# Moving the Newton steps of q's and k's norms to GpSimd and their squares to ScalarE, in a hybrid attention and RG-LRU block

## The chip, the cores and the metric

The kernel runs on one core of a Trainium2 chip. Its engines are TensorE (PE; its weight loads are listed apart as PEld), VectorE (DVE), ScalarE (ACT), GpSimd (POOL) and SyncE (SP), which issues most transfers. The metric is the device time of one execution in microseconds (us), the median over several runs. A profile is one execution recorded instruction by instruction; L92 means line 92 of the kernel.

## The reference

One transformer block over 1024 tokens of width 1024, all in float32. A normed input is projected to q, k, v (8 heads of 64) and to two LRU inputs; q and k are normed head by head; stick-breaking attention and a gated linear recurrence (RG-LRU) run side by side; their results are concatenated, projected and added to x; a squared-ReLU MLP of width 4096 follows.

```python
def rms_norm(x, g):
    xf = x.astype(jnp.float32)
    y = xf * lax.rsqrt(jnp.mean(xf * xf, axis=-1, keepdims=True) + EPS)
    return (y * g.astype(jnp.float32)).astype(x.dtype)

# in hybrid_mixer
    q = rms_norm(q.reshape(B, S, N_ATTN_HEADS, HEAD_DIM), q_norm_g)
    k = rms_norm(k.reshape(B, S, N_ATTN_HEADS, HEAD_DIM), k_norm_g)
    attn = stick_breaking_attention(q, k, v).reshape(B, S, ATTN_WIDTH)
    lru = rg_lru(xl, w_rg, b_rg, w_ig, b_ig, lam) * jax.nn.gelu(gl)
    return jnp.concatenate([attn, lru], axis=-1) @ w_out
# in reference
        x = x + hybrid_mixer(h, ...)
        x = x + sq_relu_mlp(rms_norm(x, norm2_g[l]), w_up[l], w_down[l])
```

## The kernel before

Matrices are split into a high and a low part (`float32r` each), and a product is three matmuls on them (`mm3`, L70 to L73). `lo_part` (L59, L60) makes the low part by a subtraction on VectorE or GpSimd, after a ScalarE cast has made the high part.

The span has these stages. Until about 62 us x is loaded, normed and transposed, and the projections of head pair 0 run. Then come the four column tiles of the LRU branch (`lru_tile`, L364 to L392), with reciprocals (L384) and scans (L391) on VectorE, products (L388, L389) on GpSimd and one Sqrt (L385) a tile on ScalarE, whose table set is loaded and switched back each time. From there to about 460 us a list written out by hand, `ORDER`, interleaves the attention blocks (A and three digits: head pair, head, query chunk of 256), the projections of pairs 1 to 3 (I: pair, token chunk of 256), the gates of the LRU branch (G) and sums of MLP weights by accumulating transfers issued from GpSimd's queue (Y). The output projection and the MLP, behind about 600 us, fill the second half.

The change lies in `in_proj(p, qkv, ws, tp)`, called sixteen times (four pairs, four chunks of 256 tokens). It projects 256 tokens to q, k and v of one head pair (24 matmuls for each 128 tokens). ScalarE evicts q and k to the tile `raw` (L203, two buffers) and v to `vv` (L205); VectorE makes v's low part (L206). Then comes the norm: the squares `sq` (L209) and their sums `ssq` over each head (L211, 8 columns: two token tiles by two heads of q and two of k), `rsqrt_mean` (L88 to L98), the scaling of `raw` (L213), q's gains on GpSimd (L214), and the high and low parts `qs`, `ks`, `kl` (L219 to L223). TensorE transposes these (L228, L233, L237), and ScalarE and VectorE evict them (L229, L234, L238) to `qT`, `kH` and `kL`, which the attention reads.

`rsqrt_mean` computes 1/sqrt(mean + eps) without a table: a first guess from the bits of v (L92, L93) and three Newton steps of three VectorE operations each (L95 to L97), y becoming y(1.5 - 0.5 v y y). Two other places call it, each four times: `norm1_scale` (L250) and the second norm behind the output projection (L602).

In `attention` a block of scores z goes through two sigmoids on ScalarE (L436, L437), a scan on VectorE (L441), a product on GpSimd (L442), transposes on TensorE (L452) and a split (L456, L60), to the matmuls with v (L461).

Within each engine instructions run in the order of its queue. That order is not the order of the text: the kernel is built with `tile.TileContext(nc, schedule_with_timeline_sim=True)`, which plans the queues of all engines from the dependencies and from costs of its own. In the trace, for instance, the Newton steps of one norm lie between steps of another and low parts of x.

Of the kernel before, what the change touches and what calls it, by code (L numbers as in the profile page):

```python
# [13 lines left out]
AF = mybir.ActivationFunctionType  # L14
ALU = mybir.AluOpType
# [9 lines left out]
HD = 64  # L25
# [18 lines left out]
def kernel(ctx, tc, x, norm1_g, w_in, conv_w, conv_b, w_rg, b_rg, w_ig, b_ig,  # L44
                             lam, q_norm_g, k_norm_g, w_out, norm2_g, w_up, w_down, out):
    nc = tc.nc
# [12 lines left out]
    def lo_part(eng, lo, src, hi):  # L59
        ins = eng.tensor_tensor(lo, src, hi.bitcast(F32), op=ALU.subtract)  # L60
        if eng is nc.gpsimd:
            mark(ins)
# [7 lines left out]
    def mm3(ps, ah, al, bh, bl, start, stop):  # L70
        nc.tensor.matmul(ps, al, bh, start=start, stop=False)  # L71
        nc.tensor.matmul(ps, ah, bl, start=False, stop=False)  # L72
        nc.tensor.matmul(ps, ah, bh, start=False, stop=stop)  # L73
# [10 lines left out]
    def bank(pl, shape, name):  # L84
        return pl.tile([P] + shape, F32, tag=pl.name, name=name)


    def rsqrt_mean(ssq, n, cols):  # L88
        v = small.tile([P, 8], F32, tag="rs_v", name="rs_v")[:, :cols]
        y = small.tile([P, 8], F32, tag="rs_y", name="rs_y")[:, :cols]  # L90
        m = small.tile([P, 8], F32, tag="rs_m", name="rs_m")[:, :cols]
        nc.vector.tensor_scalar(v, ssq, 1.0 / n, EPS, op0=ALU.mult, op1=ALU.add)  # L92
        nc.vector.tensor_scalar(y.bitcast(I32), v.bitcast(I32), -0.5, float(0x5F3759DF), op0=ALU.mult, op1=ALU.add)  # L93
        for _ in range(3):
            nc.vector.scalar_tensor_tensor(m, y, -0.5, v, op0=ALU.mult, op1=ALU.mult)  # L95
            nc.vector.tensor_tensor(m, m, y, op=ALU.mult)
            nc.vector.scalar_tensor_tensor(y, m, 1.5, y, op0=ALU.add, op1=ALU.mult)  # L97
        return y  # L98
# [94 lines left out]
    def in_proj(p, qkv, ws, tp):  # L193
        qT, kH, kL, vv = qkv
        raw = mp.tile([P, 2, 4, HD], F32, tag="raw", name=f"raw{p}{tp}", bufs=2)
        for tt in range(2):
            t = 2 * tp + tt
            pd = bank(ps_d, [384], f"pd{p}{t}")
            for kc in range(KC):
                wh, wl = ws[kc]  # L200
                mm3(pd, hTh[:, kc, t * P:(t + 1) * P], hTl[:, kc, t * P:(t + 1) * P], wh, wl, kc == 0, kc == KC - 1)
            rs = rstd1[:, t:t + 1]
            nc.scalar.mul(raw[:, tt].rearrange("p a d -> p (a d)"), pd[:, 0:256], rs)  # L203
            pvv = pd[:, 256:384].rearrange("p (h d) -> p h d", h=2)
            nc.scalar.mul(vv[:, t, :, 0:HD], pvv, rs)  # L205
            nc.vector.scalar_tensor_tensor(vv[:, t, :, HD:P], pvv, rs, vv[:, t, :, 0:HD].bitcast(F32), op0=ALU.mult, op1=ALU.subtract)  # L206
        sq = mp.tile([P, 8, HD], F32, tag="sq", name=f"sq{p}{tp}")
        raw8 = raw.rearrange("p t a d -> p (t a) d")
        nc.vector.tensor_tensor(sq, raw8, raw8, op=ALU.mult)  # L209
        ssq = small.tile([P, 8], F32, tag="ssq8", name=f"ssq{p}{tp}")  # L210
        nc.vector.tensor_reduce(ssq, sq, axis=AX.X, op=ALU.add)  # L211
        rstd = rsqrt_mean(ssq, HD, 8)
        nc.vector.tensor_tensor(raw8, raw8, rstd.unsqueeze(2).broadcast_to([P, 8, HD]), op=ALU.mult)  # L213
        nc.gpsimd.tensor_tensor(raw[:, :, 0:2, :], raw[:, :, 0:2, :], qkg, op=ALU.mult)  # L214
        qs = mp.tile([P, 2, 2, 2, HD], F32R, tag="qs", name=f"qs{p}{tp}")
        ks = mp.tile([P, 4, 2, HD], F32R, tag="ks", name=f"ks{p}{tp}")
        kl = mp.tile([P, 2, 2, HD], F32R, tag="kl", name=f"kl{p}{tp}")
        for h in range(2):
            nc.scalar.copy(qs[:, :, h, h, :], raw[:, :, h, :])  # L219
            lo_part(nc.vector, qs[:, :, h, 1 - h, :], raw[:, :, h, :], qs[:, :, h, h, :])  # L220
        for tt in range(2):
            nc.scalar.copy(ks[:, 2 * tt:2 * tt + 2], raw[:, tt, 2:4, :].unsqueeze(2).broadcast_to([P, 2, 2, HD]))
            lo_part(nc.gpsimd, kl[:, tt], raw[:, tt, 2:4, :], ks[:, 2 * tt:2 * tt + 2, 0, :])  # L223
        cols = slice(256 * tp, 256 * tp + 256)
        pq = bank(ps_t, [2, 256], f"pq{p}{tp}")
        for h in range(2):
            for tt in range(2):
                nc.tensor.matmul(pq[:, h, tt * P:(tt + 1) * P], qs[:, tt, h].rearrange("p a d -> p (a d)"), identr, start=True, stop=True)  # L228
        nc.scalar.copy(qT[:, :, cols], pq)  # L229
        pk = bank(ps_t, [2, 256], f"pk{p}{tp}")  # L230
        for h in range(2):
            for tt in range(2):
                nc.tensor.matmul(pk[:, h, tt * P:(tt + 1) * P], ks[:, 2 * tt + h].rearrange("p a d -> p (a d)"), identr, start=True, stop=True)  # L233
        nc.vector.tensor_copy(kH[:, :, cols], pk)  # L234
        pl = bank(ps_t, [256], f"pl{p}{tp}")
        for tt in range(2):
            nc.tensor.matmul(pl[:, tt * P:(tt + 1) * P], kl[:, tt].rearrange("p a d -> p (a d)"), identr, start=True, stop=True)  # L237
        nc.vector.tensor_copy(kL[:, cols], pl)  # L238
# [11 lines left out]
    def norm1_scale(t0, t1):  # L250
        ssq = small.tile([P, 8], F32, tag="ssq8", name=f"ssq_x{t0}")
        for t in range(t0, t1):
            junk = xp.tile([P, D], F32, tag="junk", name=f"junk{t}", bufs=2)
            nc.scalar.activation(junk, xts[t], AF.Square, accum_out=ssq[:, t - t0:t - t0 + 1])
        nc.vector.tensor_copy(rstd1[:, t0:t1], rsqrt_mean(ssq[:, :t1 - t0], D, t1 - t0))
# [39 lines left out]
    norm1_scale(2, 4)  # L295
    scale_row(0)
    in_proj(0, qkv0, wpair, 0)
    vrow = xp.tile([40, P], F32, name="vrow", bufs=1)
    nc.sync.dma_start(vrow[0:16], conv_w.rearrange("o k (c p) -> (o k c) p", p=P))
# [39 lines left out]
    for tp in range(2, NT // 2):  # L339
        load_x(2 * tp)  # L340
        load_x(2 * tp + 1)
        norm1_pair(2 * tp)
        norm1_scale(2 * tp, 2 * tp + 2)
        if tp == 3:
            scale_row(1)
        in_proj(0, qkv0, wpair, tp - 1)
    in_proj(0, qkv0, wpair, NT // 2 - 1)
    xstack.close()

# [212 lines left out]
    for n in range(2):  # L562
        wo = {}
        for grp in ((0, 1, 2), (3,), (4,), (5,), (6,), (7,)) if n == 0 else tuple((t,) for t in range(NT)):
# [20 lines left out]
            for t in grp:  # L585
                nc.sync.dma_start(x1[:, t, 512 * n:512 * n + 512], x[t * P:(t + 1) * P, 512 * n:512 * n + 512])
                xs = x1[:, t, 512 * n:512 * n + 512]
                nc.vector.tensor_tensor(xs, pos[t], xs, op=ALU.add)
                if n == 1 and t % 2:
                    for b in range(KC // 2):  # L590
                        pt = bank(ps_w, [2, 2, P], f"pth{t}_{b}")
                        for j in range(2):
                            for i in range(2):
                                nc.tensor.transpose(pt[:, j, i, :], x1[:, t - 1 + i, (2 * b + j) * P:(2 * b + j + 1) * P], ident)
                        for j in range(2):
                            kc = 2 * b + j
                            nc.scalar.mul(h2[:, kc, (t - 1) * P:(t + 1) * P], pt[:, j].rearrange("p i t -> p (i t)"), gain2[:, kc:kc + 1])
                    ssq = small.tile([P, 8], F32, tag="ssq8", name=f"ssq_h{t}")
                    for i in range(2):
                        junk = stp.tile([P, 2, 512], F32, tag="sl", name=f"junkh{t}{i}")  # L600
                        nc.scalar.activation(junk.rearrange("p a b -> p (a b)"), x1[:, t - 1 + i, :], AF.Square, accum_out=ssq[:, i:i + 1])
                    rstd = rsqrt_mean(ssq[:, :2], D, 2)  # L602
                    nc.vector.tensor_tensor(rs2[:, t - 1:t + 1], rstd, rstd, op=ALU.mult)
# [271 lines left out]
```

## Time and profile before

| | us |
|---|---|
| median of 3 runs | 1215.21 |
| lowest and highest | 1215.03 and 1216.63 |
| the profiled execution | 1218.14 |
| its span (first to last instruction) | 1216.4 |

The span is what the profile's positions in time are counted from; the time around it is 1.74 us. The mean clock that TensorE was granted is 0.969 of full speed. In a group's row stand the line, the engine, the operation, output and inputs with their shapes, the count; then busy us and mean ns of one; then the idle time of the engine just before these instructions and what ended it. In the row of a source line three durations stand for least, median and most. "Issue" in the chain of waits is time in which an engine waited for nothing that the profile shows. In a row of the timeline or of the chain the first number is the start, the second the duration.

### The profile page before, as it was taken

What the parts mean: (1) busy time and instruction counts of PE and PEld (TensorE: products, weight loads), DVE (VectorE), ACT (ScalarE), POOL (GpSimd) and SP (SyncE); (2) the same over time, 40 slices, a digit from 0 to 9 for tenths busy, and PEclk for the clock granted to TensorE, in tenths of its full rate; (3) what the DMA queues carried; (4) which work ended last, traced back from release to release, by engine and by line L of the source; (5) the groups of instructions that cost most, each with busy time, mean ns of one, the idle gap of its engine ahead of it and who ended that gap; (6) DMA issues with size and microseconds to landing.
All of it is one profiled execution on the core that took longest, in us unless ns stands there. A gap on an engine that the chain in (4) does not pass through costs nothing.

```text
span 1216.4 us, 15273 instructions
## 1 busy us (share of the span) xinstructions
PE 1150.6 (95%) x5410; PEld 948.0 (78%) x5410; DVE 897.3 (74%) x1182; ACT 568.5 (47%) x991; POOL 586.5 (48%) x472
## 2 busy tenths in 40 slices
PE   7998899999999988998999989889999999999998
PEld 7976777789987766886888767678887887878887
DVE  6889997999898788226387769685843876699663
ACT  7554475665665564144433554233334335733331
POOL 1356764574355566102645746533317368483240
PEclk9999999799999978998999989989999999999999
DMA  8110026824505275200453788944412345442531
GB/s 262 48 49 35 18 96 130 227 66 145 122 5 112 89 256 181 101 1 35 141 188 130 201 241 287 224 142 139 141 35 87 122 144 191 158 148 73 193 132 69
DMA packets 91659, 157.05 MB, mean 129 GB/s; under 512 B 8848, under 2 KB 27328, under 8 KB 91584
## 3 DMA queue, kind: packets, MB, share of 16 engines
q1 hardware_dynamic: 79040, 122.54, 30.5%
q0 software_dynamic: 12544, 33.56, 11.8%
q8 instruction: 42, 0.69, 0.2%
q14 instruction: 33, 0.27, 0.1%
HBM read 145.58 MB, written 44.04 MB: 156 GB/s over the span
## 4 chain that ended last, share of the span: by engine, by line
PE 69%; DVE 13%; issue 8%; DMA 3%; POOL 3%; ACT 3%; SPq 0%; DVEq 0%; ACTq 0%; POOLq 0%
PE p L633 22%; PE pa L633 11%; PE pb L633 5%; PE pc L633 4%; PE pd L71 3%; PE pd L72 3%; PE pd L73 3%; PE po L71 3%; PE po L72 2%; PE po L73 2%; PE av L461 2%; PE z L432 2%; PE pw L452 2%; DVE g L441 2%; DVE sl_u L60 2%
## 5 line engine op out<-in xcount | busy, mean ns | idle before, releaser
L442 POOL TENSOR_TENSOR w<-w,g 128x128 f32<-128x128 f32 (+3 forms) x96 | 99.7, 1044 | 107.7 <-DVE g L441 52.7
L60 DVE TENSOR_TENSOR ml_p<-rp,mh_p 128x1024 fp32r<-128x1024 f32 x56 | 110.3, 1971 | 28.1 <-ACT mh_p L544 28.1
L441 DVE TENSOR_TENSOR_SCAN g<-g 128x128 f32<-128x128 f32 (+3 forms) x96 | 112.6, 1185 | 8.0 <-ACT g L436 5.4
L544 ACT CAST sh_p<-U 128x1024 fp32r<-128x1024 f32 x48 | 50.5, 1051 | 131.0 <-PE pa L633 59.2
L633 PE MATMUL pa<-mh_p,sl_p 128*128 128x512 f32 x256 | 100.7, 393 | 7.1 <-DVE sl_p L60 6.8
L767 POOL TENSOR_TENSOR rp<-rp,qp 128x1024 f32<-128x1024 f32 x24 | 69.0, 2876 | 70.3 <-DMA qp<-in_w_down_dram 39.8
L633 PE MATMUL pa<-ml_p,sh_p 128*128 128x512 f32 x256 | 100.3, 392 | 0.0
L633 PE MATMUL pa<-mh_p,sh_p 128*128 128x512 f32 x256 | 100.1, 391 | 0.0
L71 PE MATMUL pd<-wh_p,hTl 128*128 128x384 f32 x256 | 90.9, 356 | 7.3 <-DVE vv L206 5.0
L72 PE MATMUL pd<-wl_p,hTh 128*128 128x384 f32 x256 | 89.8, 351 | 0.1
L73 PE MATMUL pd<-wh_p,hTh 128*128 128x384 f32 x256 | 88.3, 345 | 0.0
L60 DVE TENSOR_TENSOR sl_p<-U,sh_p 128x1024 fp32r<-128x1024 f32 x38 | 63.4, 1668 | 30.7 <-ACT sh_p L544 30.7
L737 POOL TENSOR_TENSOR ru<-ru,rv 128x1024 f32<-128x1024 f32 x16 | 43.8, 2769 | 58.9 <-DMA rv<-sum_u 58.8
L544 ACT CAST mh_p<-rp 128x1024 fp32r<-128x1024 f32 x56 | 58.7, 1048 | 21.3 <-POOL rp L767 14.6
L633 PEld LDWEIGHTS pa<-mh_p,sl_p 128*128 128x128 f32 x256 | 48.5, 189 | 18.2 <-DVE sl_p L60 7.5
L662 POOL TENSOR_TENSOR U<-U 128x512 f32<-128x512 f32 x32 | 47.0, 1501 | 32.0 <-ACT U L660 32.0
L456 ACT CAST wth<-pw 128x512 fp32r<-128x512 f32 (+1 forms) x80 | 42.4, 545 | 38.0 <-PE pw L452 24.8
L436 ACT ACTIVATE g<-z 128x384 f32<-128x384 f32 (+3 forms) x96 | 47.8, 497 | 22.9 <-PE z L434 10.4
L71 PEld LDWEIGHTS pd<-wh_p,hTl 128*128 128x128 f32 x256 | 49.4, 193 | 11.0 <-DVE vv L206 6.7
L660 ACT ACTIVATE U<-U 128x512 f32<-128x512 f32 x48 | 30.0, 628 | 58.6 <-DVE U L721 31.1
L60 DVE TENSOR_TENSOR wtl<-pw,wth 128x512 fp32r<-128x512 f32 (+1 forms) x80 | 49.5, 629 | 9.5 <-ACT wth L456 8.9
L633 PEld LDWEIGHTS pa<-mh_p,sh_p 128*128 128x128 f32 x256 | 48.5, 189 | 10.2
(325 smaller groups left out, 3566.7 us busy)
## 6 DMA issues: line engine op xcount, KB each, us to landing
sum_u<-in_w_up_dram POOLq DMA_DIRECT2D x8, 2048.0 KB, 12.7
sum_d<-in_w_down_dram POOLq DMA_DIRECT2D x8, 2048.0 KB, 13.3
rp<-in_w_down_dram SPq DMA_DIRECT2D x32, 512.0 KB, 4.1
rp<-sum_d SPq DMA_DIRECT2D x24, 512.0 KB, 5.4
ra<-in_w_up_dram SPq DMA_DIRECT2D x16, 512.0 KB, 4.4
qp<-in_w_down_dram SPq DMA_DIRECT2D x16, 512.0 KB, 4.2
wr_p<-in_w_in_dram SPq DMA_DIRECT2D x24, 192.0 KB, 5.8
xt<-in_x_dram SPq DMA_DIRECT2D x8, 512.0 KB, 7.5
```

Source lines behind the costliest of these rows:

```text
L60: ins = eng.tensor_tensor(lo, src, hi.bitcast(F32), op=ALU.subtract)
L71: nc.tensor.matmul(ps, al, bh, start=start, stop=False)
L72: nc.tensor.matmul(ps, ah, bl, start=False, stop=False)
L73: nc.tensor.matmul(ps, ah, bh, start=False, stop=stop)
L436: nc.scalar.activation(g[:, :kn], z, AF.Sigmoid, scale=-1.0)
L441: nc.vector.tensor_tensor_scan(gr, gr, gr, g[:, kn:kn + 1], op0=ALU.mult, op1=ALU.bypass)
L442: mark(nc.gpsimd.tensor_tensor(w[:, :kn], w[:, :kn], g[:, 1:kn + 1], op=ALU.mult))
L544: nc.scalar.copy(hl[0], src)
L633: nc.tensor.matmul(ps, x_, y_, start=start and n == 0, stop=stop and n == 2, skip_group_check=True)
L662: mark(nc.gpsimd.tensor_tensor(c, c, c, op=ALU.mult))
L737: mark(nc.gpsimd.tensor_tensor(r, r, q, **add))
L767: mark(nc.gpsimd.tensor_tensor(r, r, q, **add))
```

## The change

`rsqrt_mean` gets a flag. With it the first guess stays on VectorE, v is scaled by -0.5 in place on GpSimd, and each Newton step is four plain GpSimd operations in place of three VectorE ones, two of which fuse two operations. Only the call in `in_proj` sets the flag. The squares of `raw` in `in_proj` become one ScalarE activation.

```diff
-    def rsqrt_mean(ssq, n, cols):
+    def rsqrt_mean(ssq, n, cols, gp=False):
...
         nc.vector.tensor_scalar(v, ssq, 1.0 / n, EPS, op0=ALU.mult, op1=ALU.add)
         nc.vector.tensor_scalar(y.bitcast(I32), v.bitcast(I32), -0.5, float(0x5F3759DF), op0=ALU.mult, op1=ALU.add)
+        if gp:
+            nc.gpsimd.tensor_scalar(v, v, -0.5, 0.0, op0=ALU.mult, op1=ALU.add)
+            for _ in range(3):
+                nc.gpsimd.tensor_tensor(m, y, y, op=ALU.mult)
+                nc.gpsimd.tensor_tensor(m, m, v, op=ALU.mult)
+                nc.gpsimd.tensor_scalar(m, m, 1.0, 1.5, op0=ALU.mult, op1=ALU.add)
+                nc.gpsimd.tensor_tensor(y, y, m, op=ALU.mult)
+            return y
         for _ in range(3):
             nc.vector.scalar_tensor_tensor(m, y, -0.5, v, op0=ALU.mult, op1=ALU.mult)
...
-        nc.vector.tensor_tensor(sq, raw8, raw8, op=ALU.mult)
+        nc.scalar.activation(sq, raw8, AF.Square)
         ssq = small.tile([P, 8], F32, tag="ssq8", name=f"ssq{p}{tp}")
         nc.vector.tensor_reduce(ssq, sq, axis=AX.X, op=ALU.add)
-        rstd = rsqrt_mean(ssq, HD, 8)
+        rstd = rsqrt_mean(ssq, HD, 8, True)
```

## The prediction

> **What bounds the kernel now.** I read the busy shares of the page first, then the busy time of each engine by stretches, then the chain of work that ended last inside the stretches where TensorE isn't full.
>
> ```profile
> span 1216.4 us, 15273 instructions
> ...
> PE 1150.6 (95%) x5410; PEld 948.0 (78%) x5410; DVE 897.3 (74%) x1182; ACT 568.5 (47%) x991; POOL 586.5 (48%) x472
> ```
> ```profile
> 100.00:150.00 50.00, 41.01 (x189) 32.74 (x188) 49.48 (x51) 24.86 (x38) 32.45 (x26) 0.99 0.08 32
> ...
> 250.00:300.00 50.00, 50.00 (x305) 44.25 (x303) 47.42 (x90) 30.63 (x75) 31.22 (x39) 1.00 0.34 114
> ...
> 350.00:400.00 50.00, 48.28 (x272) 40.10 (x271) 42.90 (x84) 29.37 (x76) 29.12 (x46) 0.97 0.34 70
> ...
> 600.00:1216.00 616.00, 589.98 (x2557) 483.64 (x2556) 429.11 (x322) 244.69 (x286) 300.15 (x131) 0.98 0.49 153
> ```
>
> The columns of a stretch are its ends, its length, then the busy time of PE, PEld, DVE, ACT and POOL, the granted clock, and DMA. Over the whole span TensorE is the bound, but the change touches only the sixteen norms of q and k, which run before 400 us; the 616 us behind 600 hold none of them and I count no change there. What matters is how the norms' stretches differ. From 250 to 300 TensorE is busy for all 50 us: DVE work taken away there buys nothing. From 100 to 150 it is VectorE that is full (49.48 of 50) while TensorE is busy for 41.01; from 350 to 400 TensorE has 1.7 us idle and fewer weight loads (271 against 303). In the first 62 us, where the four norms of pair 0 lie, I also count nothing: what they wait for is work that TensorE's own projections and transposes cover. So a gain has to come from the LRU stretch (to about 155 us) and the attention stretches around 180 and 360 to 390.
>
> **The change part by part: what leaves VectorE.**
>
> ```profile
> L209 DVE TENSOR_TENSOR sq<-raw 128x512 f32<-128x512 f32 x16 | 14.4, 901 | 4.7 <-ACT raw L203 4.7
> ...
> L96 DVE TENSOR_TENSOR rs_m<-rs_m,rs_y 128x8 f32<-128x8 f32 x48 | 12.4, 260 | 0.9
> ...
> L97 DVE SCALAR_TENSOR_TENSOR rs_y<-rs_m,rs_y 128x8 f32<-128x8 f32 x48 | 11.4, 238 | 0.9
> ...
> L95 DVE SCALAR_TENSOR_TENSOR rs_m<-rs_y,rs_v 128x8 f32<-128x8 f32 x48 | 10.1, 212 | 0.9
> ```
>
> Sixteen squares (14.4 us) and 144 Newton operations (12.4 + 11.4 + 10.1 = 33.9 us) leave: 48.3 us of DVE busy time. The two operations that prepare v and y (L92, L93) and the reduction (L211) stay on VectorE. Only what stands on the chain counts:
>
> ```profile
> 130.99 1.43 issue
> ...
> 144.83 0.06 DVE rs_m L96
> 144.89 1.03 issue
> ...
> 147.06 1.16 DVE rs_y L97
> 148.21 0.60 DVE sq L209
> ...
> 151.62 0.20 DVE rs_m L95 x2
> 151.82 0.20 DVE rs_m L96 x2
> 152.02 0.20 DVE rs_y L97 x2
> ```
> ```profile
> 174.62 0.87 DVE sq L209
> ...
> 181.10 0.14 DVE rs_m L95
> ...
> 183.89 0.18 DVE rs_y L97
> ```
> ```profile
> 361.59 0.65 DVE sq L209
> ...
> 365.25 1.91 DVE g L441
> ...
> 367.45 0.97 DVE rs_m L96
> ...
> 369.05 0.18 DVE rs_y L97
> ...
> 380.21 1.08 issue
> ...
> 383.36 0.18 DVE rs_m L95
> ...
> 385.99 1.01 DVE g L441
> 387.00 0.06 DVE rs_y L97
> ```
>
> These are rows of the chain (start, us, what). The "issue" at 130.99 lies inside a square and that at 144.89 inside an L96. (1) LRU stretch: squares 1.43 + 0.60, with small pieces 2.2 us; Newton 0.06 + 1.03 + 1.16, with small pieces 2.5 us. Here the chain follows VectorE's queue: the LRU's reciprocals and scans stand behind these operations, so what leaves is gained. (2) 174 to 184: square 0.87; nine Newton operations from 181.10 to 183.89, 1.5 us, nearly back to back, each waiting for the one before. (3) 361 to 369: square 0.65, Newton 2.05 (the 0.97 in it). (4) 380 to 387: square 1.1, Newton 1.2 in nine pieces from 383.36 to 387.00, with other DVE work (the scan of 1.01 and evictions) between them. With the second Newton chain of the LRU stretch, 0.20 + 0.20 + 0.20 us at 151.62 and small pieces, 0.7 in all, that is 4.8 us of squares and 8.0 us of Newton, 12.8 us at most, in six norms.
>
> **What ScalarE gets.**
>
> ```profile
> L385 ACT ACT_TABLE_LOAD x4 | 5.1, 1283 | 0.1
> ...
> L488 ACT ACTIVATE ge<-gx 128x512 f32<-128x512 f32 x8 | 5.0, 631 | 8.2 <-DVE gx L487 7.7 <-POOL w L442 0.4
> ```
>
> L488 is a Square of just this shape: 0.63 us, sixteen times 10.1 us, on an engine that is busy for 24.86 of 50 us in the LRU stretch and 29.37 around 375. The reduction now waits for ScalarE instead of for DVE's square: where the chain goes through the norm itself, (2), (3) and (4), 0.63 us comes back each time, 1.9 us. Behind a Square on ScalarE stand the sigmoids of the next attention block; 0.63 us is covered by its idle half. In the LRU stretch ScalarE switches table sets (1283 ns a load); no Square of the trace runs under the Sqrt's set, so a reload is possible there, a rival below. The Trainium skill, "ScalarE: Activation LUTs", section "Table sets", says that cheap functions such as copy and identity stand in every set, and doesn't name Square among them; by it the reload is unlikely, and no run so far shows it.
>
> **What GpSimd gets.** Per norm 13 operations of 128x8: one scaling of v, then three steps of three products and one addition; 208 in all. None is in the trace.
>
> ```profile
> L404 POOL COPY ext<-ext x4: 187/187/627, 66.4 to 113.0; 128x3 f32<-128x3 f32 x4
> ```
> ```profile
> L442 POOL TENSOR_TENSOR w<-w,g 128x128 f32<-128x128 f32 x16 | 8.3, 520 | 16.1 <-DVE rs_y L97 7.6 <-DVE g L441 3.8 <-DVE rs_m L95 2.3
> ```
> ```profile
> 127.26 1.28 POOL L388 TENSOR_TENSOR rg<-rg,ext 128x512 f32<-128x512 f32 x1 [1.45 <-DVE ext L384]
> 128.62 1.29 POOL L389 TENSOR_TENSOR ig<-ig,rg 128x512 f32<-128x512 f32 x1
> ```
>
> Lower bound 0.187 us (three columns, one input, the median), upper 0.52 us (128 columns, two inputs, the mean). Eight columns are nearer to three, so I take 0.26 us, between that median and the mean of the four copies, (3 x 187 + 627)/4 = 297 ns. A dependent operation starts 0.08 us after the end of its source (127.26 + 1.28 = 128.54, then 128.62). A chain of 13 is 13 x (0.26 + 0.08) = 4.4 us, with the ends 3.5 and 7.8; busy 54 us in sixteen norms, beside POOL's 32.45 of 50 in the LRU stretch. On DVE the same chain took from 1.7 us (nine at 0.18 and the small gaps, back to back) upward.
>
> The upper end has a mechanism:
>
> ```profile
> 144.56 1.42 POOL L388 TENSOR_TENSOR rg<-rg,ext 128x512 f32<-128x512 f32 x1 [2.25 <-DVE rs_m L95]
> ...
> 144.75 1.25 DVE L96 TENSOR_TENSOR rs_m<-rs_m,rs_y 128x8 f32<-128x8 f32 x1
> ```
>
> An operation on 8 columns takes 1.25 us because it overlaps a GpSimd product; the same line's neighbours cost 0.18 elsewhere. This is why the Newton steps hurt DVE, and it works in the other direction too: a small GpSimd operation that meets a DVE scan can wait for it. The Trainium skill, "SBUF — State Buffer", section "Who interferes with whom", says that a DVE instruction with two SBUF inputs and a GpSimd one that reads SBUF exclude each other for the whole instruction, whoever is first. By it each of thirteen operations may wait for one scan, which speaks against this change; the trace agrees from DVE's side.
>
> New waits: GpSimd's first Newton operation waits for DVE's L93, and behind it in GpSimd's queue stand the attention's products (L442), the LRU's L388 and L389 and the issues of the weight sums. DVE's scaling L213 now waits for GpSimd; behind it in DVE's queue stand scans, lo parts and evictions, for which TensorE waits. The order within each queue comes from a planner, so where L213 ends up is not readable here.
>
> **The sum.** (1) 2.2 + 2.5 less what GpSimd's own LRU products are pushed back: its idle gap of 2.25 us (row at 144.56) takes half of a 4.4 us chain, the rest may delay L388; I take 1.0. Gain 3.7. (2) and (3): the chain is the norm's own dependency; DVE gives 1.5 and 2.05 away and is free for its next work, GpSimd answers later; I take nothing. (4) DVE has other work between its pieces: 1.2 + 1.1 - 0.63 = 1.7. Together 5.4 us. The profiled execution took 1218.14 us (span 1216.4 and 1.74 around it), so 1212.7 like it; the median of the three runs is 2.93 lower, so **1209.8, say 1210 us**.
>
> **The rivals.**
> - *The relief comes in full*: DVE always has other work while GpSimd iterates: 12.8 - 1.9 = 10.9 us, 1204. For it: DVE is full in the LRU stretch and a scan of 1.91 us stands between Newton pieces at 365.25. Against: the back-to-back run to 183.89, where it had nothing else.
> - *Given back*: at (2) and (3) the norm's own latency decides and GpSimd's chain is 4.4 - 1.7 = 2.7 us longer each: 5.4 - 5.4 = 0, 1215.
> - *Slower: DVE's queue stands at L213.* Where L213 is put right behind L93, DVE idles for GpSimd's whole chain, 4.4 us, with scans and evictions behind it. In all six norms that is 26.4 - 10.9 = 15.5 us lost, in four 17.6 - 10.9 = 6.7, 1222. It decides from 10.9/4.4 = 2.5 norms on; a chain of 7.8 us needs only 1.4 norms. For it: an in-order queue and a chain over twice as long. Against: in the order before, at (4), other DVE work lies between dependent operations (the scan of 1.01 at 385.99), so the planner fills such waits.
> - *A table reload*: two Squares in the Sqrt's set, two loads each: 4 x 1.28 = 5.1 us, the gain is gone, 1215.
>
> **How the numbers follow.** Forecast (1206 to 1212) 0.40, full relief 0.13, given back 0.20, standing queue 0.22, reload 0.05. A measurement of this kernel tells 0.2% (2.4 us) from no change, so faster is 0.40 + 0.13 = 0.53, same 0.20 + 0.05 = 0.25, slower 0.22. The range reaches below the full relief and just past the standing queue in four norms: 1201 to 1223. The far end, 1231, is left out.
>
> **What would show it.** Right: DVE busy near 850 us, POOL near 640, ACT near 579; the stretch 100 to 150 with TensorE over 43; L213 seldom idle for GpSimd; small GpSimd operations at 0.2 to 0.3 us; the time from L92 to L213 not longer than before. Wrong: DVE idle ahead of L213 released by GpSimd, several us in sum; means near 0.5 us; L442 or TensorE's weight loads waiting for Newton lines; more table loads; or a reordering by the planner that moves the idle time of TensorE in stretches that the change doesn't touch.

## The result and the profile after

The changed kernel takes **1226.81 us** in the median of four runs (1224.53 to 1231.76), the kernel before 1215.12 us on the same chip: a ratio of 1.0100, with a 95% interval of 1.0066 to 1.0134. It is slower by 11.7 us, where 1210 us was forecast. The profiled execution took 1228.02 us (span 1226.2).

The page of the changed kernel, span and busy times:

```profile
span 1226.2 us, 15289 instructions
...
PE 1151.0 (94%) x5410; PEld 948.0 (77%) x5410; DVE 867.1 (71%) x1022; ACT 576.2 (47%) x1007; POOL 641.6 (52%) x680
```

VectorE has 160 instructions less, but only 30.2 us less busy time (897.3 before), not 48.3: some of what is left on it became longer, the scaling of `raw` for one (865 ns in the mean, 691 before). POOL and ACT are where the prediction put them. The same four stretches as in the prediction (ends, length, then busy PE, PEld, DVE, ACT, POOL, clock, DMA):

```profile
100.00:150.00 50.00, 41.73 (x174) 33.19 (x173) 49.03 (x46) 26.93 (x41) 35.96 (x40) 0.88 0.08 32
250.00:300.00 50.00, 48.04 (x282) 40.91 (x281) 39.50 (x63) 30.16 (x71) 40.49 (x66) 1.00 0.21 70
350.00:400.00 50.00, 50.00 (x282) 40.91 (x281) 39.55 (x60) 31.86 (x81) 38.15 (x76) 1.00 0.33 63
600.00:1216.00 616.00, 590.33 (x2559) 484.38 (x2558) 428.09 (x319) 246.49 (x289) 299.61 (x134) 0.98 0.50 154
```

From 100 to 150 VectorE is as full as before, though squares and Newton steps have left it; TensorE's granted clock is 0.88 there instead of 0.99, and its busy time holds fewer matmuls (174, before 189). And from 250 to 300, where TensorE had no idle time at all, it now has 2 us. New groups of the changed kernel between 20 and 470 us (the lines of `in_proj` stand 8 higher than before: L217 is the Square, L221 the scaling of `raw`; L95 scales v on GpSimd, L97 to L100 are the steps), and behind them the scaling in the kernel before:

```profile
L99 POOL TENSOR_SCALAR rs_m<-rs_m 128x8 f32<-128x8 f32 x48 | 13.9, 290 | 3.2
L221 DVE TENSOR_TENSOR raw<-raw,rs_y 128x512 f32<-128x512 f32 x16 | 13.8, 865 | 13.2 <-POOL rs_y L100 12.8 <-POOL g L443 0.3
...
L217 ACT ACTIVATE sq<-raw 128x512 f32<-128x512 f32 x16 | 10.3, 647 | 0.0
L95 POOL TENSOR_SCALAR rs_v<-rs_v 128x8 f32<-128x8 f32 x16 | 7.3, 459 | 25.2 <-DVE rs_y L93 23.5 <-DVE sp L341 1.4
```
```profile
L213 DVE TENSOR_TENSOR raw<-raw,rs_y 128x512 f32<-128x512 f32 x16 | 11.1, 691 | 0.3
```

Two waits are new: VectorE stands 13.2 us at the scaling (0.3 before), GpSimd 25.2 us at the first step. GpSimd's is in part idle time that stood elsewhere, since ahead of the attention's product w it fell from 107.7 to 61.6 us. And the chain of waits, which in the kernel before ran through VectorE's Newton steps, now runs through GpSimd's:

```profile
162.28 0.14 DVE rs_v L92
...
163.51 0.08 DVE rs_y L93
...
164.82 0.11 POOL rs_m L97
164.93 1.07 POOL w L450
166.00 0.29 POOL rs_m L98
...
167.75 1.21 POOL rs_m L99
...
170.16 0.20 POOL rs_y L100
```

This norm, the seventh of sixteen, takes 8.1 us from L92 to its scaling at 170.40; in the kernel before it took 5.6 (161.62 to 167.23). The attention's product (w) stands between the steps in the planner's order, and one step of 0.20 us takes 1.21. In the last twelve norms the steps take 4.2 to 13.1 us from first to last, 7.0 in the mean; the prediction had 4.4, at most 7.8. A good place to measure the stretch as a whole is its last eviction of the attention's output (kernel before, then changed kernel; durations least, median, most, then first and last start):

```profile
L467 DVE TENSOR_TENSOR ob<-av,ot x32: 386/422/428, 169.7 to 461.5; 64x256 f32<-64x256 f32 x32
```
```profile
L475 DVE TENSOR_TENSOR ob<-av,ot x32: 387/422/429, 172.8 to 467.2; 64x256 f32<-64x256 f32 x32
```

So 5.7 of the 9.8 us between the two spans are lost before 468 us. The rest comes after it, where the change has no instruction and all queues have the same order in both kernels: 754.9 us from that eviction to the end before, 759.0 after. Over all 17 profiled executions of this study, whatever the kernel, this remainder lies between 754.6 and 759.7 us. I read the 4 us as that spread; what makes it was not tried. The granted clock doesn't explain the first part: from 0 to 450 us it is 0.96 in both kernels, and in the runs below it doesn't go with the time (e5: 0.94, attention over at 460.3; e6: 0.96, at 486.6).

### The profile page after: what moved, and what is told of

It is laid out like the page before. It is cut to its first block, busy times and chain, and to the rows that moved or that the text cites. A ratio compares the mean times of both kernels' runs of the same rounds, so it can differ in the third digit from the quotient of the medians.

```text
span 1226.2 us, 15289 instructions
## 1 busy us (share of the span) xinstructions
PE 1151.0 (94%) x5410; PEld 948.0 (77%) x5410; DVE 867.1 (71%) x1022; ACT 576.2 (47%) x1007; POOL 641.6 (52%) x680
## 3 DMA queue, kind: packets, MB, share of 16 engines
q0 software_dynamic: 12544, 33.56, 11.7%
## 4 chain that ended last, share of the span: by engine, by line
PE 67%; DVE 12%; issue 8%; POOL 5%; ACT 4%; DMA 4%; SPq 0%; DVEq 0%; POOLq 0%; ACTq 0%
PE p L641 21%; PE pa L641 11%; PE pb L641 5%; PE pc L641 4%; PE po L71 2%; PE av L469 2%; PE po L72 2%; PE po L73 2%; PE pw L460 2%; PE pd L71 2%; PE pd L73 2%; PE pd L72 2%; PE z L440 2%; DVE g L449 1%; DVE sl_p L60 1%
## 5 line engine op out<-in xcount | busy, mean ns | idle before, releaser
L450 POOL TENSOR_TENSOR w<-w,g 128x128 f32<-128x128 f32 (+3 forms) x96 | 100.6, 1059 | 61.6 <-DVE g L449 27.8
L60 DVE TENSOR_TENSOR ml_p<-rp,mh_p 128x1024 fp32r<-128x1024 f32 x56 | 112.8, 2015 | 27.5 <-ACT mh_p L552 27.5
L552 ACT CAST mh_p<-rp 128x1024 fp32r<-128x1024 f32 x56 | 58.6, 1047 | 24.9 <-POOL rp L775 17.3
L670 POOL TENSOR_TENSOR U<-U 128x512 f32<-128x512 f32 x32 | 46.6, 1491 | 31.1 <-ACT U L668 31.1
L60 DVE TENSOR_TENSOR wtl<-pw,wth 128x512 fp32r<-128x512 f32 (+1 forms) x80 | 49.2, 626 | 14.3 <-ACT wth L464 13.6
L460 PE MATMUL pw<-ident,w 128*128 128x128 f32 x288 | 49.7, 293 | 7.4 <-DVE wtl L60 6.2
## 6 DMA issues: line engine op xcount, KB each, us to landing
sum_d<-in_w_down_dram POOLq DMA_DIRECT2D x8, 2048.0 KB, 12.7
```

The lines of the kernel that those rows point to most:

```text
L450: mark(nc.gpsimd.tensor_tensor(w[:, :kn], w[:, :kn], g[:, 1:kn + 1], op=ALU.mult))
L460: nc.tensor.transpose(pw[:, i * P:(i + 1) * P], wrow[rr][j // 4][:, j % 4 * P:(j % 4 + 1) * P], ident)
L552: nc.scalar.copy(hl[0], src)
L670: mark(nc.gpsimd.tensor_tensor(c, c, c, op=ALU.mult))
```

## The experiments

Since the planner places every instruction anew when a kernel changes, a difference of times mixes two things: the operations and the order. To part them, most of the kernels here were given a fixed order: an edge "issue after" (no wait, no semaphore) from each instruction to its neighbour in its engine's queue, for all five engines, with the order of the kernel before, or of the changed one, taken from its built program. In their traces the instructions of VectorE, ScalarE, GpSimd and SyncE that both kernels share do stand in that order.

```diff
+def _pin(tc, nc, mybir, orders):
...
+            if prev is not None:
+                tc.add_manual_dep(seq[at], prev.name, mybir.DependencyInfo(mybir.DependencyClass.NoSync, mybir.DependencyReason.DATA), reason="order")
+            prev = seq[at]
...
         tile_hybrid_block_kernel(tc, *args)
+        _pin(tc, nc, _mybir, _ORDERS)
```

All results in one table. "Old" is the queue order of the kernel before, "new" that of the changed kernel, "free" the planner's own for that kernel. A GpSimd chain in the old order stands together where the norm's first VectorE step stood ("early") or its last ("late"). The kernel before, timed beside each group, had medians of 1214.34 to 1216.9 us; so kernels of different groups are compared by their ratios, and the last but one column is the ratio less 1, times 1216 us. The last eviction is that of the one profiled execution.

| run | square; Newton operations a norm | order | median us | ratio to before (95%) | us against before | last eviction, us |
|---|---|---|---|---|---|---|
| before | VectorE; 9 VectorE | old | 1215.12 | | 0 | 461.5 |
| after | ScalarE; 13 GpSimd | free = new | 1226.81 | 1.0100 (1.0066 to 1.0134) | +12.2 | 467.2 |
| e1 | ScalarE; 13 GpSimd, early | old | 1228.45 | 1.0100 (1.0074 to 1.0127) | +12.2 | 471.2 |
| e2 | VectorE; 9 VectorE | new | 1242.91 | 1.0235 (1.0208 to 1.0261) | +28.6 | 488.6 |
| e3 | ScalarE; 9 VectorE | free | 1242.56 | 1.0235 (1.0209 to 1.0261) | +28.6 | 486.1 |
| e4 | VectorE; 13 GpSimd | free | 1246.69 | 1.0256 (1.0226 to 1.0286) | +31.1 | 488.1 |
| e5 | ScalarE; 9 VectorE | old | 1216.25 | 0.9989 (0.9966 to 1.0011) | -1.3 | 460.3 |
| e6 | VectorE; 13 GpSimd, late | old | 1248.66 | 1.0259 (1.0231 to 1.0288) | +31.5 | 486.6 |
| e7 | ScalarE; 13 GpSimd, late | old | 1241.16 | 1.0205 (1.0178 to 1.0233) | +24.9 | 482.7 |
| e8 | as before, two copies swapped | free | 1229.30 | 1.0112 (1.0081 to 1.0144) | +13.6 | 473.3 |
| e9 | ScalarE; none | old | 1208.45 | 0.9959 (0.9941 to 0.9978) | -5.0 | 453.2 |
| e10 | ScalarE; 5 GpSimd, late | old | 1212.96 | 0.9976 (0.9957 to 0.9994) | -2.9 | 457.0 |
| e11 | ScalarE; 6 VectorE | old | 1214.45 | 0.9971 (0.9950 to 0.9992) | -3.5 | 455.3 |
| e12 | as e7, scaling on GpSimd too | old | 1244.41 | 1.0238 (1.0221 to 1.0256) | +28.9 | 486.8 |
| e13 | ScalarE; 9 GpSimd, late | old | 1225.01 | 1.0071 (1.0045 to 1.0098) | +8.6 | 466.2 |
| e14 | ScalarE; 5 GpSimd | free | 1221.27 | 1.0036 (1.0016 to 1.0056) | +4.4 | 461.2 |
| e15 | ScalarE; none | free | 1222.66 | 1.0048 (1.0029 to 1.0068) | +5.8 | 465.3 |

### Operations against order: e1 and e2

Edit: the fixed order alone, added to the changed kernel (e1) and to the kernel before (e2).

> All of the changed kernel's operations, held on every engine in the queue order that the kernel before had: each Square stands where VectorE's square stood, the 13 GpSimd steps of a norm stand together where its nine VectorE steps began; every other instruction keeps its place (the kernel before's 5394 TensorE, 967 ScalarE, 470 GpSimd, 397 SyncE and 1022 remaining VectorE entries, none moved). Theory A (the operations cost: VectorE stands at the scaling of raw for 13 blocked GpSimd steps, 12.8 us of such waits in the trace of after): this kernel is as slow as the changed one or slower, 1222 to 1232 us, and VectorE shows 10 us or more of waits for GpSimd ahead of that line. Theory B (the planner's new order costs, not the operations): 1206 to 1214 us, what the prediction summed for an order that stays. Half of each: about 1217 to 1221 us.

> All of the kernel before's operations (squares and Newton steps on VectorE), held on every engine in the queue order that the changed kernel had: each norm's nine VectorE steps stand together at the place of its first GpSimd step, the square at that of the Square. Theory A (the operations cost): the time of the kernel before, 1212 to 1218 us. Theory B (the order costs): the time of the changed kernel, 1222 to 1232 us, or more, since VectorE has 30 us more to do in an order that was made for less.

Both theories hold, and they don't add up. With the order kept, the operations cost 12.2 us (and VectorE stands 18.0 us at the scaling). With the operations kept, the new order, made for other operations, costs 28.6 us. Both together cost 12.2: the new order is bad for the old operations, and for the new ones as good as the old. In e1 one sees what a chain on another queue does. Timeline of e1, VectorE, GpSimd and ScalarE:

```profile
153.19 0.69 DVE L221 TENSOR_TENSOR raw<-raw,rs_y 128x512 f32<-128x512 f32 x1
153.38 0.56 POOL L95 TENSOR_SCALAR rs_v<-rs_v 128x8 f32<-128x8 f32 x1 [2.43 <-DVE rs_y L93]
...
157.00 0.20 POOL L100 TENSOR_TENSOR rs_y<-rs_y,rs_m 128x8 f32<-128x8 f32 x1
157.16 0.72 POOL L222 TENSOR_TENSOR raw<-raw,qkg 128x256 f32<-128x256 f32 x1
157.84 0.87 POOL L60 TENSOR_TENSOR kl<-raw,ks 128x128 fp32r<-128x128 f32 x2
157.91 0.50 ACT L227 CAST qs<-raw 128x128 fp32r<-128x128 f32 x2 [3.29 <-POOL raw L222]
```

The scaling at 153.19 belongs to one norm, the thirteen steps behind it to the next. The first norm's gains (L222) stand in GpSimd's queue behind the second norm's chain and come at 157.16; its cast `qs` has waited 3.29 us for them.

### The halves, with a free order and with the old one: e3 to e6

> The squares on ScalarE alone, the Newton steps back on VectorE, the planner free. 16 squares of 900 ns leave VectorE, 16 of 647 ns come to ScalarE; no wait for GpSimd is added. Theory A: 1211 to 1215 us, and the loss of the change is all in its other half. Theory B (order): the planner moves the order again, and the time may land anywhere between 1208 and 1230 us, with no relation to what was moved.

> The Newton steps on GpSimd alone, the squares back on VectorE, the planner free. Theory A: the whole loss is here, 1222 to 1230 us, with VectorE waiting for GpSimd ahead of the scaling of raw for about 12 us in all. Theory B: the planner moves the order in another way, and the time may land anywhere between 1208 and 1230 us; with an order as good as before's it is 1212 to 1216 us.

Edits: in the changed kernel the flag taken away (e3) or the square put back on VectorE (e4).

```diff
-        rstd = rsqrt_mean(ssq, HD, 8, True)
+        rstd = rsqrt_mean(ssq, HD, 8)
```
```diff
-        nc.scalar.activation(sq, raw8, AF.Square)
+        nc.vector.tensor_tensor(sq, raw8, raw8, op=ALU.mult)
```

Each half costs more than the whole, and more than either theory gave it: 28.6 and 31.1 us. Taken alone, e3 would say that the Square is ruinous. Held in the old order the two halves say something else.

> The squares on ScalarE alone, and every queue held in the order of the kernel before; each Square stands at the place of the square that it replaces. Theory B' (a new order alone made the square-only kernel of the first four runs 28 us slower; the Square itself costs nothing): 1209 to 1216 us. Theory A' (the Square on ScalarE is itself what costs): 1225 us or more.

> The Newton steps on GpSimd alone, every queue held in the order of the kernel before; a norm's 13 GpSimd steps stand where its last VectorE step stood, so behind all that GpSimd did before then, and VectorE's scaling of raw keeps its place. Theory A' (each norm comes later by the GpSimd chain of about 3.6 us, against some 1.5 to 2 us for nine VectorE steps, and what waits for it waits too): 1222 to 1230 us. Theory B' (only orders cost): 1208 to 1216 us.

The Square costs nothing that can be measured: a ratio of 0.9989 (0.9966 to 1.0011). All of e3's 28.6 us are its order. The Newton steps are not free: 31.5 us with the order kept, more than Theory A' said; and in e4, the same operations in the planner's own order, they cost as much (31.1).

### Where the chain stands in GpSimd's queue, and how long it is: e7, e10, e13, e9

> All of the changed kernel's operations in the order of the kernel before, as in the first run, but each norm's 13 GpSimd steps stand at the place of its last VectorE step rather than of its first. In the first run's trace one norm's chain stood in GpSimd's queue ahead of the previous norm's multiplication by the gains, which came 4.2 us later for it at 158 us. If the first run's 14 us came from such places in the queue: 1208 to 1218 us. If they come from the chain's length itself (theory A'): 1222 to 1230 us.

> The three Newton steps of q's and k's norms are left out (so their scale is only the first guess); Squares on ScalarE, every queue in the order of the kernel before. Beside the run with the Squares alone (1216.25 us) it takes 9 VectorE steps out of each of 16 norms and puts nothing in their place: what relieving VectorE of them is worth at most. By the prediction's terms, 8.0 us of Newton work on the path: about 1208 us. If that work lies beside other work: 1213 to 1217 us.

> As the seventh run (13 GpSimd steps a norm, at the place of the last VectorE step, 1241.16 us), but with one Newton step in place of three, so 5 GpSimd operations a norm; two steps are left out of the computation. Theory C (the length of the chain on each norm's path costs): between the run without steps (Z) and the seventh in proportion to the operations, Z + 5/13 of the distance: about 1221 us if Z is 1208, 1225 if Z is 1216. Theory X (to cross to GpSimd at all costs: the place in its queue and the two hand-overs): 1233 to 1241 us.

> As the seventh and tenth runs, with two Newton steps on GpSimd, 9 operations a norm (the third step is left out of the computation). Five operations gave 1212.96 us and 22.2 us of VectorE standing at the scaling of raw; thirteen gave 1241.16 us and 51.2 us. Theory C with a slack (a norm may come about 1.5 us later for nearly nothing, and from there on each microsecond of chain comes back in the time almost whole): halfway, 1224 to 1230 us, with some 37 us of standing. Rival (one place tips over, somewhere between 5 and 13 operations): either 1213 to 1218 or 1236 to 1241 us.

Edits: for e7 the fixed order alone; for the others, in the changed kernel, the count of steps, for e9 none at all.

```diff
-            for _ in range(3):
+            for _ in range(1):
                 nc.gpsimd.tensor_tensor(m, y, y, op=ALU.mult)
```

From 0 over 5 and 9 to 13 operations the time against the kernel before goes -5.0, -2.9, +8.6, +24.9 us: 0.4, 2.9 and 4.1 us for each further operation (in all sixteen norms). Sixteen operations spaced 0.28 us are 4.5 us: the last ones come back nearly whole, the first ones hardly. So e10 is far below the 1221 us of a cost in proportion, e7 is above what was expected for a long chain, and e13 lies near the middle between them, as a steady cost behind a slack would have it; nothing tips over at one place. The group of the scaling in e10, e13 and e7, in this order:

```profile
L221 DVE TENSOR_TENSOR raw<-raw,rs_y 128x512 f32<-128x512 f32 x16 | 11.7, 734 | 22.2 <-POOL rs_y L100 16.1 <-POOL g L443 6.1
```
```profile
L221 DVE TENSOR_TENSOR raw<-raw,rs_y 128x512 f32<-128x512 f32 x16 | 13.1, 817 | 35.6 <-POOL rs_y L100 26.2 <-POOL g L443 9.4
```
```profile
L221 DVE TENSOR_TENSOR raw<-raw,rs_y 128x512 f32<-128x512 f32 x16 | 13.1, 818 | 51.2 <-POOL rs_y L100 38.4 <-POOL g L443 12.8
```

VectorE stands 22.2 us in e10 and the kernel is not slower than the kernel before; from there to e7 it stands 29.0 us longer and the attention ends 25.7 us later (457.0 and 482.7). The run with nine VectorE operations, e5, lies between 5 and 9 GpSimd operations: at 5 + 4 x 1.6 / 11.5 = 5.6 by the times (-2.9, -1.3, +8.6), at 5 + 4 x 3.3 / 9.2 = 6.4 by the last evictions (457.0, 460.3, 466.2). The interval of e5, 4.1 us gained to 1.3 lost, leaves this wide.

In the old order, the price of a chain at that place follows when the norm is ready. The time from the end of the first guess (L93) to the start of the scaling, in the mean of the last twelve norms, is:

| run | before | e9 | e5 | e10 | e13 | e7 |
|---|---|---|---|---|---|---|
| L93 to scaling, us | 5.2 | 3.7 | 5.3 | 5.4 | 6.4 | 7.6 |
| us against before | 0 | -5.0 | -1.3 | -2.9 | +8.6 | +24.9 |

So e10 and e5 break even in this time, though not in the bare length of their chains (5 steps take 1.2 us on GpSimd; on VectorE the nine of the seventh to the sixteenth norm in the kernel before take 3.0 to 6.1 us from first to last, because other work lies between them). From e10 to e7 a norm comes 2.3 us later (5.35 and 7.61), twelve norms 27 us, and the kernel is 27.8 us slower. From e5 to e9 it comes 1.6 us earlier, twelve norms 19 us, and the kernel gains 3.7 (7.1 by the last evictions). **Lateness comes back nearly whole, earliness hardly.** The sum holds only there. In e1 this time is 5.8 us, and the 12.2 us lost are more than it gives: there the chains also hold up the gains of the norm ahead. In the changed kernel, with its own order, it is 7.6 us as in e7, at half of e7's price.

Here is how the long chain adds up. The scaling of four norms in the kernel before, and the same four in e7, whose queues have the same order:

```profile
62.29 0.69 DVE L213 TENSOR_TENSOR raw<-raw,rs_y 128x512 f32<-128x512 f32 x1
...
167.23 0.69 DVE L213 TENSOR_TENSOR raw<-raw,rs_y 128x512 f32<-128x512 f32 x1
...
274.42 0.17 DVE L97 SCALAR_TENSOR_TENSOR rs_y<-rs_m,rs_y 128x8 f32<-128x8 f32 x1
274.62 0.69 DVE L213 TENSOR_TENSOR raw<-raw,rs_y 128x512 f32<-128x512 f32 x1
...
369.25 0.69 DVE L213 TENSOR_TENSOR raw<-raw,rs_y 128x512 f32<-128x512 f32 x1
```
```profile
66.05 0.69 DVE L221 TENSOR_TENSOR raw<-raw,rs_y 128x512 f32<-128x512 f32 x1 [1.66 <-POOL rs_y L100]
...
176.66 1.57 DVE L221 TENSOR_TENSOR raw<-raw,rs_y 128x512 f32<-128x512 f32 x1 [2.00 <-POOL rs_y L100]
...
282.76 0.15 DVE L447 COPY g<-g 128x1 f32<-128x1 f32 x1
288.13 0.69 DVE L221 TENSOR_TENSOR raw<-raw,rs_y 128x512 f32<-128x512 f32 x1 [5.21 <-POOL rs_y L100]
...
393.28 0.69 DVE L221 TENSOR_TENSOR raw<-raw,rs_y 128x512 f32<-128x512 f32 x1 [5.22 <-POOL g L443]
```

It is a staircase: 3.8 us late, then 9.4, 13.5, 24.0. Ten norms in a row, the sixth to the fifteenth, add 1.2 to 3.0 us each, also from 250 to 300, where TensorE had been busy throughout. What VectorE waits for at 288.13 is on GpSimd:

```profile
281.72 2.94 POOL L450 TENSOR_TENSOR w<-w,g 128x512 f32<-128x512 f32 x2 [2.48 <-DVE g L449]
284.64 0.19 POOL L95 TENSOR_SCALAR rs_v<-rs_v 128x8 f32<-128x8 f32 x1
...
287.90 0.20 POOL L100 TENSOR_TENSOR rs_y<-rs_y,rs_m 128x8 f32<-128x8 f32 x1
```

First two products of the attention that stand ahead, then 3.46 us of steps. In the kernel before, VectorE had put its own steps between scans and low parts, and the norm was ready when its turn came. A rival is that the steps hold up the attention's products behind them on GpSimd. The waits of other engines for these products speak against it (5.3 us in all in the kernel before, 6.1 in e7), but no run adds work to GpSimd without making the norm later.

### Is it VectorE's standing? e12

> As the seventh run (1241.16 us), but the scaling of raw by the norm (128x512) is issued on GpSimd too, behind the 13 steps, so that VectorE no longer has an instruction in its queue that waits for the chain and goes on with what stands behind it. The scaling takes longer there (1.3 us or more, 0.7 us on VectorE), so each norm itself comes 0.6 us or more later. Theory S (what costs is VectorE standing in order at that line): 1222 to 1236 us. Theory C (what costs is that the norm, and all that is made from it, comes later): as before or more, 1241 to 1253 us.

```diff
-        nc.vector.tensor_tensor(raw8, raw8, rstd.unsqueeze(2).broadcast_to([P, 8, HD]), op=ALU.mult)
+        nc.gpsimd.tensor_tensor(raw8, raw8, rstd.unsqueeze(2).broadcast_to([P, 8, HD]), op=ALU.mult)
```

Not settled. VectorE has no wait at the scaling any more, 51.2 us of standing there are gone, and the kernel is no faster than e7 (+28.9 against +24.9 us). But VectorE still stands for the norm, one line further on: at the low parts of q, which wait for ScalarE's casts of the scaled `raw`, and these for GpSimd (waiter, releaser, us, times, longest; e7, then e12):

```profile
DVE qs L60 <- ACT qs L227: 3.9, 4, 1.4
DVE wtl L60 <- ACT wth L464: 9.1, 13, 1.3
```
```profile
DVE qs L60 <- ACT qs L227: 30.0, 8, 5.8
DVE wtl L60 <- ACT wth L464: 20.4, 21, 4.3
```

The norm itself is also later: its scaling takes 1056 ns on GpSimd (818 on VectorE in e7), and from the eviction of `raw` to its end 14.8 us pass instead of 13.5, in the mean of the last twelve norms. At the price above that would have been some 15 us, and 4.0 were found. So e12 shows that the wait at the scaling is not the whole price, and not that VectorE's standing costs nothing. In both runs VectorE stands for the late norm.

### Is a new order by itself a loss? e8, e14, e15

> The kernel before with no operation moved to another engine and none added: only the two ScalarE copies of a projection's bank, that of q and k and that of v, are written in the other order, and the planner is free. It then puts 1118 of 5394 TensorE, 266 of 967 ScalarE and 297 of 1022 VectorE entries (Newton steps and squares not counted) at other places in their queues. Theory B' (orders that differ from the one of the kernel before cost, whatever is changed): 1225 to 1245 us. Theory A' (operations cost, an order is worth little): 1211 to 1219 us.

> The kernel of the tenth run (Squares on ScalarE, one Newton step as 5 GpSimd operations, two steps left out; 1212.96 us in the order of the kernel before), now with the planner free to order. Theory B'' (a new order costs by itself, whatever the chain): 1222 to 1240 us. Rival (the planner's order costs only where it has to plan around a long chain): 1209 to 1217 us.

> The kernel of the ninth run (Squares on ScalarE, all three Newton steps left out; 1208.45 us in the order of the kernel before), now with the planner free to order. Theory B'': 1218 to 1236 us, though VectorE has less to do than in any other run and GpSimd nothing more. Rival: 1205 to 1212 us.

Edit of e8, in the kernel before; e14 and e15 are e10 and e9 without the fixed order.

```diff
-            nc.scalar.mul(raw[:, tt].rearrange("p a d -> p (a d)"), pd[:, 0:256], rs)
             pvv = pd[:, 256:384].rearrange("p (h d) -> p h d", h=2)
             nc.scalar.mul(vv[:, t, :, 0:HD], pvv, rs)
+            nc.scalar.mul(raw[:, tt].rearrange("p a d -> p (a d)"), pd[:, 0:256], rs)
```

Often, not always. Two copies written in the other order, and the kernel is 13.6 us slower. With the same operations, the free order costs 7.3 us with one step (+4.4 against -2.9) and 10.8 us with none (+5.8 against -5.0). A kernel that leaves the whole Newton work out is slower than the kernel before if the planner orders it. With the long chain the planner's order costs nothing (e4 against e6, 31.1 and 31.5; the changed kernel against e1, 12.2 both) or even gains (against e7). The rival of e14 and e15, an order that costs only around a long chain, is the opposite of what was found; e14 itself lies just below the range that its theory gave. The windows from 200 to 250 and from 250 to 300 us, e9 (old order), then e15 (free):

```profile
200.00:250.00 50.00, 46.94 (x235) 35.95 (x235) 43.77 (x65) 32.73 (x77) 26.02 (x43) 0.86 0.71 176
250.00:300.00 50.00, 49.94 (x304) 44.03 (x303) 43.09 (x69) 31.70 (x77) 32.44 (x41) 1.00 0.33 114
```
```profile
200.00:250.00 50.00, 43.56 (x226) 33.98 (x224) 38.42 (x52) 29.50 (x69) 24.74 (x33) 0.90 0.71 178
250.00:300.00 50.00, 45.36 (x235) 37.33 (x236) 43.20 (x65) 30.20 (x73) 29.37 (x42) 0.86 0.26 71
```

TensorE is idle 8.0 us more in these 100 us, of the 12.1 us by which the attention ends later; its clock is also lower there in e15 (0.90 and 0.86, against 0.86 and 1.00). Which moved entry of the queues does it was not followed up.

### Less of the work where it was: e11

> The Newton work stays on VectorE but with two steps in place of three, with constants fitted to the first guess (relative error worked out at 6e-7), so 6 VectorE operations a norm in place of 9; Squares on ScalarE; every queue in the order of the kernel before. If the steps' length is on the path: a third of what the run without steps gains, so 1211 to 1214 us where that is 1208. If not: 1215 to 1217 us, the run with the Squares alone.

```diff
+            for a_, c_ in ((-0.50318345, 1.504038), (-0.50000028, 1.5000008)):
+                nc.vector.scalar_tensor_tensor(m, y, a_, v, op0=ALU.mult, op1=ALU.mult)
+                nc.vector.tensor_tensor(m, m, y, op=ALU.mult)
+                nc.vector.scalar_tensor_tensor(y, m, c_, y, op0=ALU.add, op1=ALU.mult)
```

The first guess's constant goes with them (0x5F370000). A ratio of 0.9971 (0.9950 to 0.9992) to the kernel before, 1214.45 us: a shorter chain on the same engine, in the same order, is the one version with the whole computation that is faster than both kernels clear of noise, by three tenths of a per cent. Against e5 alone, which differs only in the steps, it is 2.2 us, and the two intervals overlap. The attention ends at 455.3 us, between e5's 460.3 and e9's 453.2.

## Why the prediction was wrong

**What held.** The durations: a Square takes 647 ns (0.63 forecast), and 13.9 + 12.3 + 12.0 + 11.8 + 7.3 = 57.3 us of steps came to GpSimd (54 forecast). A lone step takes 0.20 us and the next starts 0.28 us behind it (284.64 to 287.90 is twelve spacings, 0.27 each), so the chain is 3.5 us where nothing stands between, not 4.4. No table load came with the Square (9 loads before and after). The worth of the Newton work on the path was put at 8.0 us; leaving it out in the old order gained 3.7 us by the times of e5 and e9 (-1.3 and -5.0) and 7.1 us by their last evictions (460.3 and 453.2).

**The step that failed** is the sum's "(2) and (3): ... GpSimd answers later; I take nothing", and the count under it, "12.8 us at most, in six norms" (its rows hold five squares, so five norms). The chain of waits shows what is late now. A norm that is just in time is not on it, so the norms off the chain, eleven of sixteen, were given no price for coming later, and (2) and (3) none either. In the changed kernel the time from L93 to the scaling is 7.6 us in the mean of the last twelve norms, 5.2 before. In e7, with the order kept as the sum assumed, the sixth to the fifteenth norm add their steps to the staircase, and the kernel loses 24.9 us instead of gaining 5.4; in e1, with the chains placed better, it still loses 12.2. "From 250 to 300 TensorE is busy for all 50 us: DVE work taken away there buys nothing" is right for work taken away; it was then used as if a delay there cost nothing either, and two steps of that staircase are the norms that the kernel before scaled in this stretch, at 274.62 and 291.51 us.

**The second failure** is the order. The prediction named the planner, said that the place of L213 could not be read, and listed a reordering among the signs, but put no price on it and let the sum stand for an order that stays. In five pairs the other order cost 7 to 30 us with the operations unchanged (e15 against e9, e14 against e10, e8 and e2 against before, e3 against e5); in two, with the long GpSimd chain, nothing (e4 against e6, the changed kernel against e1). For the changed kernel itself the two causes can't be split into a sum: its order recovers nothing of what the operations cost in the old order with the chains placed early, 12.7 us with them placed late; and that order costs 28.6 us with the old operations.

**The squares.** The term 4.8 - 1.9 = 2.9 us isn't refuted: e5 measures 1.3 us of gain, with an interval from 4.1 gained to 1.3 lost. Beside late chains the Square may be worth more, 6.6 us between e6 and e7, whose intervals just touch; this was not followed up.

**The rivals.** "Given back" had the right mechanism, the norm's own latency, but in two norms with 2.7 us each; in e7 the last twelve norms are 2.4 us slower from L93 to the scaling, and ten in a row add to the staircase. "DVE's queue stands at L213" came nearest with 1222 us, and VectorE does stand, 13.2 us in the changed kernel, 51.2 in e7. How much of the price is that standing is open, since e12 only moves it one line on. Its objection, "the planner fills such waits", is true, and worth little: the changed kernel stands less than e1 (13.2 against 18.0 us) and is no faster. "Full relief", a gain of 10.9 us, wasn't reached even by e9, which has no chain at all (5.0 us gained). The reload did not occur.

## What to carry to other kernels

A chain of short dependent operations is moved at the price of how much later its result is ready, not of its busy time. Count the steps, multiply by the spacing on the new engine, add what stands ahead of them in its queue and between them, and compare with the time that the old chain takes in place. Charge the difference at every place where the result is used, also where the chain of waits doesn't pass and where TensorE is full, for a view of what is late says nothing of what is just in time. Where a planner orders the queues, time a change a second time with the order of the kernel before held fixed; without that, a Square that costs nothing measurable looked like 28.6 us. Shortening a chain where it stands (nine operations to six) was worth a little here; moving it cost.

## What was not expected of the hardware

- GpSimd is quicker on tiny operations than was taken: 0.19 to 0.20 us for 128x8, one input or two, and 0.28 us from one dependent start to the next, against 0.17 and 0.20 us on VectorE (268.53 and 268.73 in the kernel before). What makes the chain long is the spacing and the number, 13 for 9, and in the changed kernel what stands between the steps.
- A GpSimd product seems to be held off by several VectorE instructions one after the other. Timeline of the changed kernel, GpSimd, then VectorE:

```profile
254.32 5.16 POOL L499 TENSOR_TENSOR hl<-hl,gx 128x512 f32<-128x512 f32 x1
254.45 1.26 DVE L449 TENSOR_TENSOR_SCAN g<-g 128x512 f32<-128x512 f32 x1
255.64 0.66 DVE L497 SCALAR_TENSOR_TENSOR ge<-ge,gx 128x512 f32<-128x512 f32 x1
256.23 2.17 DVE L449 TENSOR_TENSOR_SCAN g<-g 128x512 f32<-128x512 f32 x2
```

  The product takes 5.16 us, where its like takes 1.27 (the next, from 259.48), and VectorE's instructions have their usual durations. They fill 254.45 to 258.40; 5.16 less these 3.95 us is 1.21, about the product's usual time. The Trainium skill, "SBUF — State Buffer", section "Who interferes with whom", says that issue order decides who blocks whom. By the recorded starts the product was first (254.32 against 254.45) and still lost, and it lost against a run of instructions, not one; this is one instance, and no run here tells how exact the recorded start is.
